# Every fifth weight operand of the first half in ScalarE's two copy tiles, and one accumulation there on VectorE

## The chip, the core and the metric

The kernel runs on one core of a Trainium2 chip. The core has a matrix engine (PE, with its weight loads shown apart as PEld), a vector engine (DVE), a scalar engine (ACT), GpSimd (POOL), and SyncE (SP), on whose queue all of this kernel's transfers are issued. The engines run side by side, each in its own fixed order of instructions, and wait for one another through semaphores. The metric is the time of one execution on the device, in microseconds (us).

## What is computed

A residual trunk of one layer over 2048 tokens of width 1024, in float32. Two mixers run on the normalised input and are projected back; that takes the first 540 us or so and the change leaves it alone. Then comes the SwiGLU block, 2816 wide, and a final norm:

```
h = rmsnorm(h_res, norm_ffn_g[l])
ff = jax.nn.silu(h @ ffn_w1[l]) * (h @ ffn_w3[l])
h_res = h_res + ff @ ffn_w2[l]
return rmsnorm(h_res, final_norm_g)
```

## The kernel before, in words

**Two halves.** The 2048 tokens are four chunks of 512. The SwiGLU block runs twice, over two chunks each: the first half (`hf == 0`) and the second (`hf == 1`). All that follows is about the first half.

**Seven products instead of eight.** Each 2x2 block product is formed by Strassen-Winograd's scheme: seven products per 2x2 block, with sums and differences of the weight quarters (`t1` to `t4`, made on POOL by `comb`, lines 605 and 703) and of the activations. There are eleven blocks of the inner width (`NP`, index `j`). For a block, `ffn1` runs twice (gate and up, tiles `ps`, operands `h_hi`, `h_lo`) and `ffn2` once (tiles `pY`, `pX`, `pZ`, `pV`, operands `f_hi`, `f_lo`). In the loop, `ffn_up(j)` comes first, and then `ffn2(j)` and `ffn_gate(j + 1)` step in turn, so one pass of the loop, here called a cycle, is 21 products of 12 matmuls each. Ten such cycles follow each other.

**Two float32 parts.** Each operand is split into a rounded part and a rest: `split` copies on ACT (line 226) and subtracts on DVE (line 236). A product uses three matmuls per tile (`mm3`, lines 239 to 241): high by high, high by low, low by high. The third needs the weight's low part, so it waits for DVE.

**Where split weights live.** In the first half a weight operand is loaded raw (`load_raw`, line 210, six buffers) or combined on POOL, then split by `split_kept` into a tile `w_hl` that holds both parts. This ring (`wsp`) has four buffers: a fifth split can start only when PE has finished the product four operands back. The split is also stored to DRAM (line 205, 512 KB) for the second half, which reads it back. `t3` and `t4` go through a tag with one buffer (`r1`): the next of them can be formed only when DVE has split the one before.

**The two tiles of ACT's copies.** The tag `e` has two buffers of 512 columns. In `add` (line 712 on), a product's bank is added to its accumulator either by DVE straight from the bank (line 715, `by == "V"`), or by an ACT copy into a tile `e` and a POOL addition (line 719, `by == "P"`). In the first half of the kernel before, only the fifth product of `ffn2` (tiles `pZ`, accumulator `G`) goes by ACT and POOL.

**What sets the order.** A scheduler puts the instructions of each engine in order ahead of the run, from priorities, dependences and its own costs. Weight splits are given priority (`AHEAD`), so they stand as early as a buffer is free. The order of a queue is then fixed; an instruction that waits holds up all behind it on its engine.

Of the kernel before, what the change touches and what calls it, by code (L numbers as in the profile page):

```python
# [9 lines left out]
F32 = mybir.dt.float32  # L10
F32R = mybir.dt.float32r
# [6 lines left out]
P = 128  # L18
# [17 lines left out]
AHEAD = 400  # L36
# [36 lines left out]
def trunk(ctx: ExitStack, tc: tile.TileContext, xT, w_io, w13, w2, gates, pool_w, w_inT, vecs,  # L73
          consts, outT):
    nc = tc.nc
# [90 lines left out]
    c13_d = dram.tile([NP, 2, 7, P, 2, W], F32, name="c13_d")  # L166
    c2_d = dram.tile([NP, 7, P, 2, W], F32, name="c2_d")
# [8 lines left out]
    def t2(name, tag, shape=(P, T), dt=F32):  # L176
        return pool.tile(list(shape), dt, name=name, tag="t2_" + tag, bufs=N_T2[tag])

    def wsp(name, shape):
        return pool.tile(list(shape), F32R, name=name, tag="wsp", bufs=N_WSP)  # L180
# [3 lines left out]
    def kept(cache):  # L184


        n_kept[0] += 1
        if n_kept[0] % 7 in (1, 3, 5):
            parts = []
            for i in range(2):  # L190
                t = pool.tile([P, W], F32, name="w_kept", tag="raw", bufs=N_RAW)
                nc.sync.dma_start(t, cache[:, i])
                parts.append(t.bitcast(F32R))
            return parts
        t = pool.tile([P, 2, W], F32, name="w_kept2", tag="wsp", bufs=N_WSP)
        nc.sync.dma_start(t, cache)
        t = t.bitcast(F32R)
        return t[:, 0], t[:, 1]

    def split_kept(src, cache, prepare=AHEAD, eng=None):  # L200

        w_ = wsp("w_hl", (P, 2, W))
        with tc.high_priority(prepare):
            split(w_[:, 0], w_[:, 1], src, eng)
        nc.sync.dma_start(cache, w_.bitcast(F32))
        return w_[:, 0], w_[:, 1]
# [6 lines left out]
    def bank(name):  # L213
        return psum.tile([P, T], F32, name=name, tag="mm", bufs=4)
# [10 lines left out]
    def copy_a(out, in_):  # L225
        return nc.scalar.activation(out, in_, AF.Copy)  # L226
# [6 lines left out]
    def split(hi, lo, src, eng=None):  # L233

        copy_a(hi, src)
        (eng or nc.vector).tensor_tensor(lo, src, hi.bitcast(F32), ALU.subtract)  # L236
# [356 lines left out]
    def ffn1(hf, j, w, ops, s, after):  # L593
# [12 lines left out]
            return t  # L606

        def product(n, ps, a, b, fresh):
            wh, wl = split_kept(b, c13_d[j, w, n]) if hf == 0 else kept(c13_d[j, w, n])
            for kk in range(NB):  # L610
                col = slice(kk * P, kk * P + P)
                mm3(ps, wh[:, col], wl[:, col], a[0][:, kk], a[1][:, kk],
                    fresh and kk == 0, kk == NB - 1, skip_group_check=True)
# [23 lines left out]
        Z, V = bank("ps"), bank("ps")  # L637
# [52 lines left out]
    def ffn2(hf, j, s, acc, G):  # L690
# [13 lines left out]
            return t  # L704

        def product(n, banks, a, b, fresh):
            wh, wl = split_kept(b, c2_d[j, n]) if hf == 0 else kept(c2_d[j, n])
            for dp, ps in enumerate(banks):
                col = slice(P * dp, P * (dp + 1))
                mm3(ps, wh[:, col], wl[:, col], a[0], a[1], fresh, True, skip_group_check=True)  # L710

        def add(banks, dst, by):
            for dp, ps in enumerate(banks):
                if by == "V":
                    nc.vector.tensor_tensor(dst[dp], ps, dst[dp], ALU.add)  # L715
                else:
                    e = t2("e", "e")
                    copy_a(e, ps)
                    nc.gpsimd.tensor_tensor(dst[dp], dst[dp], e, ALU.add)  # L719
# [11 lines left out]
        g = [G[:, dp] for dp in range(NB)]  # L731
# [26 lines left out]
        s2 = half(ALU.subtract, s1, a11)  # L758
        Z = banks("pZ")
        product(4, Z, operand(s2), tt2, True)  # L760
        add(Z, g, "P")
        yield
        V = banks("pV")
        product(5, V, operand(s1), t1, True)
# [207 lines left out]
```

## Time and profile before

| what | value |
|---|---|
| median of 3 runs | 1911.29 us (1910.66 to 1914.16) |
| profiled execution, its own time | 1915.5 us |
| its span, first to last instruction | 1913.7 us |
| PE busy | 1826.2 us, 95% |
| DVE busy | 1350.9 us, 71% |
| ACT busy | 728.8 us, 38% |
| POOL busy | 803.6 us, 42% |

The busy shares are means over stages that differ: the first half of the SwiGLU block lies between about 549 and 1240 us, the second between about 1240 and 1862 us. PE's busy time counts an instruction from start to end, and matmuls overlap, so the number of matmuls in a stretch tells more of its speed than the busy share. Times in the rows are microseconds from the span's start; a row's bracket is the idle time of its engine just before and what ended it.

### The profile page before, as it was taken

Reading aid. Unit: us, or ns where it says so; the run is one execution under the profiler, and the core shown is the slowest. Engines: PE = TensorE matmul, PEld = TensorE weight load, DVE = VectorE, ACT = ScalarE, POOL = GpSimd, SP = SyncE. Lnnn points to the kernel's source line nnn. Section 1 sums busy time; section 2 is a strip of 40 time slices with the busy share of each in tenths; the row PEclk is TensorE's granted clock in tenths of the full one; section 3 lists DMA queues with packets and bytes.
Section 4 is the critical chain, followed back from the end, with each engine's and each line's share of the span. In section 5 each row is a group of like instructions: output and inputs, shape, how many; then the busy total and the mean of one; then the engine's idle time right before and its main releaser. Section 6 shows DMA issues by size and latency. Waiting matters only on the chain.

```text
span 1913.7 us, 23347 instructions
## 1 busy us (share of the span) xinstructions
PE 1826.2 (95%) x8016; PEld 1479.8 (77%) x8016; DVE 1350.9 (71%) x2080; ACT 728.8 (38%) x1216; POOL 803.6 (42%) x557
## 2 busy tenths in 40 slices
PE   7998999999988999999999999799999999999996
PEld 5787887787767777778777787678888888888885
DVE  7588599895768779878898778984544554544558
ACT  5554546352334434333343334532322223322223
POOL 3361623342234545345453556352433333433373
PEclk9999999999989999999999999899999999999998
DMA  9874954576987676666766667777555555555542
GB/s 322 316 254 171 345 207 168 176 269 238 362 330 288 218 257 226 235 228 239 257 228 227 229 240 274 294 226 280 194 192 198 192 193 183 194 197 190 198 172 88
DMA packets 160837, 444.68 MB, mean 232 GB/s; under 512 B 17872, under 2 KB 20048, under 8 KB 155728
## 3 DMA queue, kind: packets, MB, share of 16 engines
q1 hardware_dynamic: 160720, 443.20, 65.2%
q8 instruction: 63, 1.03, 0.2%
q14 instruction: 54, 0.44, 0.1%
HBM read 275.36 MB, written 167.77 MB: 232 GB/s over the span
## 4 chain that ended last, share of the span: by engine, by line
PE 66%; DVE 21%; DMA 5%; issue 4%; POOL 2%; ACT 1%; SPq 0%; DVEq 0%; ACTq 0%; POOLq 0%
PE ps L241 15%; PE ps L239 15%; PE ps L240 15%; DVE w_hl L236 2%; PE pV L239 2%; PE pV L240 2%; PE pX L240 2%; PE pX L239 2%; PE pX L241 2%; PE pV L241 2%; DMA w_kept<-cio_d 1%; DVE sf L728 1%; DVE h_lo L236 1%; DVE xc L424 1%; DVE acc L715 1%
## 5 line engine op out<-in xcount | busy, mean ns | idle before, releaser
L241 PE MATMUL ps<-h_hi,w_hl 128*128 128x512 f32 x616 | 246.5, 401 | 15.8 <-DVE w_hl L236 15.4
L239 PE MATMUL ps<-h_hi,w_hl 128*128 128x512 f32 x616 | 244.5, 399 | 13.9 <-DVE u L645 9.4
L239 PE MATMUL ps<-h_hi,w_kept 128*128 128x512 f32 x616 | 241.8, 393 | 4.4 <-DVE sf L728 1.9
L240 PE MATMUL ps<-h_lo,w_hl 128*128 128x512 f32 x616 | 244.1, 396 | 0.0
L240 PE MATMUL ps<-h_lo,w_kept 128*128 128x512 f32 x616 | 241.4, 392 | 2.1 <-DVE h_lo L236 2.1
L241 PE MATMUL ps<-h_hi,w_kept 128*128 128x512 f32 x616 | 239.3, 392 | 0.0
L719 POOL TENSOR_TENSOR G<-G,e 128x512 f32<-128x512 f32 x116 | 168.5, 1476 | 107.0 <-ACT e L226 107.0
L295 POOL TENSOR_TENSOR sq<-sq 128x512 f32<-128x512 f32 (+1 forms) x71 | 103.7, 1465 | 158.1 <-ACT sq L292 156.4
L641 POOL TENSOR_TENSOR u<-u,u 128x512 f32<-128x512 f32 x44 | 66.8, 1517 | 227.7 <-DVE u L639 227.6
L241 PEld LDWEIGHTS ps<-h_hi,w_hl 128*128 128x128 f32 x616 | 117.6, 191 | 51.0 <-DVE w_hl L236 25.6
L239 PEld LDWEIGHTS ps<-h_hi,w_hl 128*128 128x128 f32 x616 | 117.7, 191 | 44.9 <-ACT w_hl L226 9.4
L236 DVE TENSOR_TENSOR f_lo<-sf,f_hi 128x512 fp32r<-128x512 f32 x80 | 75.3, 942 | 105.6 <-PE pZ L240 41.5
L605 POOL TENSOR_TENSOR t<-raw 128x512 f32<-128x512 f32 x44 | 65.7, 1497 | 186.0 <-DVE w_hl L236 92.3
L239 PEld LDWEIGHTS ps<-h_hi,w_kept 128*128 128x128 f32 x616 | 116.1, 188 | 31.2 <-DVE sf L728 2.3
L715 DVE TENSOR_TENSOR acc<-pV,acc 128x512 f32<-128x512 f32 x160 | 106.5, 687 | 46.7 <-PE pV L241 46.2
L240 PEld LDWEIGHTS ps<-h_lo,w_hl 128*128 128x128 f32 x616 | 117.7, 191 | 25.3 <-DVE h_lo L236 0.2
L240 PEld LDWEIGHTS ps<-h_lo,w_kept 128*128 128x128 f32 x616 | 116.0, 188 | 27.5 <-DVE h_lo L236 2.5
L241 PEld LDWEIGHTS ps<-h_hi,w_kept 128*128 128x128 f32 x616 | 116.1, 188 | 25.5 <-DMA w_kept<-c_d 0.3
L236 DVE TENSOR_TENSOR w_hl<-raw,w_hl 128x512 fp32r<-128x512 f32 x120 | 120.4, 1005 | 19.1 <-ACT w_hl L226 17.6
L226 ACT ACTIVATE f_hi<-sf 128x512 fp32r<-128x512 f32 x80 | 50.1, 627 | 188.2 <-DVE sf L728 150.6
L226 ACT ACTIVATE w_hl<-t 128x512 fp32r<-128x512 f32 x96 | 60.5, 630 | 145.8 <-PE ps L241 55.4
L226 ACT ACTIVATE w_hl<-raw 128x512 fp32r<-128x512 f32 x140 | 85.7, 623 | 77.4 <-PE ps L241 59.4
(359 smaller groups left out, 4499.3 us busy)
## 6 DMA issues: line engine op xcount, KB each, us to landing
c_d<-w_hl SPq DMA_DIRECT2D x228, 512.0 KB, 2.9
w_kept<-c_d SPq DMA_DIRECT2D x130, 512.0 KB, 3.6
w_kept<-c_d SPq DMA_DIRECT2D x196, 256.0 KB, 3.4
w_kept<-cio_d SPq DMA_DIRECT2D x68, 512.0 KB, 3.7
raw<-w SPq DMA_DIRECT2D x132, 256.0 KB, 3.3
w_kept<-cio_d SPq DMA_DIRECT2D x104, 256.0 KB, 3.2
cio_d<-w_hl SPq DMA_DIRECT2D x40, 512.0 KB, 4.9
h_lo<-h_d SPq DMA_DIRECT2D x14, 1024.0 KB, 9.8
```

Source lines behind the costliest of these rows:

```text
L226: return nc.scalar.activation(out, in_, AF.Copy)
L236: (eng or nc.vector).tensor_tensor(lo, src, hi.bitcast(F32), ALU.subtract)
L239: i = nc.tensor.matmul(ps, wh, xh, start=first, stop=False, **kw)
L240: nc.tensor.matmul(ps, wh, xl, start=False, stop=False, **kw)
L241: nc.tensor.matmul(ps, wl, xh, start=False, stop=last, **kw)
L295: eng.tensor_tensor(total, total, sq, ALU.add)
L424: nc.vector.scalar_tensor_tensor(x[:, d:], u[:, 0:T - d], tap(3 - d), x[:, d:], ALU.mult, ALU.add)
L605: nc.gpsimd.tensor_tensor(t, a, b, ALU.subtract)
L641: nc.gpsimd.tensor_tensor(u3, u3, u2, ALU.add)
L715: nc.vector.tensor_tensor(dst[dp], ps, dst[dp], ALU.add)
L719: nc.gpsimd.tensor_tensor(dst[dp], dst[dp], e, ALU.add)
L728: nc.vector.tensor_tensor(out, a, b, op)
```

## The change

Of the operands that `ffn1` and `ffn2` split in the first half, every fifth now goes into two tiles of the tag `e`, one for each part, and is stored by two transfers of 256 KB. The accumulation of `pZ` into `G`, which used those tiles, is done there by DVE from the bank.

```diff
-    def split_kept(src, cache, prepare=AHEAD, eng=None):
+    n_split = [0]
+
+    def split_kept(src, cache, prepare=AHEAD, eng=None, five=False):
+        n_split[0] += five
+        if five and n_split[0] % 5 == 0:
+            parts = t2("w_e", "e", dt=F32R), t2("w_e", "e", dt=F32R)
+            with tc.high_priority(prepare):
+                split(*parts, src, eng)
+            for i, part in enumerate(parts):
+                nc.sync.dma_start(cache[:, i], part.bitcast(F32))
+            return parts
...
-            wh, wl = split_kept(b, c13_d[j, w, n]) if hf == 0 else kept(c13_d[j, w, n])
+            wh, wl = split_kept(b, c13_d[j, w, n], five=True) if hf == 0 else kept(c13_d[j, w, n])
...
-            wh, wl = split_kept(b, c2_d[j, n]) if hf == 0 else kept(c2_d[j, n])
+            wh, wl = split_kept(b, c2_d[j, n], five=True) if hf == 0 else kept(c2_d[j, n])
...
-        add(Z, g, "P")
+        add(Z, g, "P" if hf else "V")
```

The scheduler orders the first half anew; up to it every engine's order is the same. In the changed kernel the lines behind `split_kept` have numbers higher by 11, so line 236 is 247 there. Three places follow.

DVE in the cycle whose `ffn_up` ends near 778 us. Before, the last two rows ahead of these are `u_6714<-ps` (the addition at line 639) and the split of the first combined weight of `ffn2`, `t_6854`. `t_6910` is the second one's, `t_6936` that of the gate product that runs beside them:

```order
L679 TENSOR_TENSOR c<-ps,u_6714 128x512
L236 TENSOR_TENSOR w_hl<-raw,w_hl 128x512
L680 TENSOR_TENSOR s<-s,c 128x512
L645 TENSOR_TENSOR u_6738<-ps,u_6738 128x512
L728 TENSOR_TENSOR sf<-s 128x512
L236 TENSOR_TENSOR f_lo<-sf,f_hi 128x512
L236 TENSOR_TENSOR w_hl<-t_6910,w_hl 128x512
L728 TENSOR_TENSOR sf<-s 128x512
L236 TENSOR_TENSOR f_lo<-s,f_hi 128x512
L728 TENSOR_TENSOR sf<-sf,s 128x512
L679 TENSOR_TENSOR u_6714<-ps,u_6714 128x512
L236 TENSOR_TENSOR w_hl<-t_6936,w_hl 128x512
```

The same place now, where the three combined weights are `t_6860`, `t_6916` and `t_6944`, and the addition is `u_6718<-ps`:

```order
L247 TENSOR_TENSOR w_hl<-t_6860,w_hl 128x512
L650 TENSOR_TENSOR u_6718<-ps,u_6718 128x512
L247 TENSOR_TENSOR w_e<-t_6916,w_e 128x512
L690 TENSOR_TENSOR c<-ps,u_6718 128x512
L247 TENSOR_TENSOR w_hl<-raw,w_hl 128x512
L691 TENSOR_TENSOR s<-s,c 128x512
L739 TENSOR_TENSOR sf<-s 128x512
L656 TENSOR_TENSOR u_6742<-ps,u_6742 128x512
L247 TENSOR_TENSOR w_hl<-t_6944,w_hl 128x512
```

The first combined weight has moved ahead of the addition, and the gate product's weight stands seven rows behind the addition, where it stood thirteen behind. The first row of `acc<-pY` stands sixteen rows behind the addition in both.

DVE where `pZ` and `pV` are accumulated, one cycle later. Before:

```order
L639 TENSOR_TENSOR u_6896<-ps,u_6896 128x512
L236 TENSOR_TENSOR w_hl<-raw,w_hl 128x512
L666 TENSOR_TENSOR s<-ps,u_6896 128x512
L236 TENSOR_TENSOR f_lo<-sf,f_hi 128x512
L236 TENSOR_TENSOR w_hl<-raw,w_hl 128x512
L645 TENSOR_TENSOR u_6954<-ps,u_6954 128x512
L715 TENSOR_TENSOR acc<-pV,acc 128x512
L236 TENSOR_TENSOR w_hl<-raw,w_hl 128x512
```

And now:

```order
L247 TENSOR_TENSOR w_e<-raw,w_e 128x512
L677 TENSOR_TENSOR s<-ps,u_6902 128x512
L247 TENSOR_TENSOR w_hl<-raw,w_hl 128x512
L726 TENSOR_TENSOR G<-pZ,G 128x512 x3
L656 TENSOR_TENSOR u_6962<-ps,u_6962 128x512
L247 TENSOR_TENSOR f_lo<-sf,f_hi 128x512
L726 TENSOR_TENSOR G<-pZ,G 128x512
L247 TENSOR_TENSOR w_hl<-raw,w_hl 128x512
L726 TENSOR_TENSOR acc<-pV,acc 128x512
```

Four additions have come in ahead of the first `acc<-pV`.

POOL at the end of the loop, where `fold` (line 774) adds `G` to twelve accumulator tiles and the last block's combined weights (`t_10302`, `t_10341`, `t__10343`, `t_10345`) are formed. Before:

```order
L641 TENSOR_TENSOR u_10014<-u_10014,u_9956 128x512
L719 TENSOR_TENSOR G<-G,e 128x512 x2
L774 TENSOR_TENSOR acc<-acc,G 128x512
L719 TENSOR_TENSOR G<-G,e 128x512
L774 TENSOR_TENSOR acc<-acc,G 128x512
L719 TENSOR_TENSOR G<-G,e 128x512
L774 TENSOR_TENSOR acc<-acc,G 128x512 x6
L605 TENSOR_TENSOR t_10345<-raw,t__10343 128x512
```

And now:

```order
L616 TENSOR_TENSOR t__10351<-raw,t_10349 128x512
L652 TENSOR_TENSOR u_10024<-u_10024,u_9966 128x512
L785 TENSOR_TENSOR acc<-acc,G 128x512 x8
L616 TENSOR_TENSOR t_10353<-raw,t__10351 128x512
L785 TENSOR_TENSOR acc<-acc,G 128x512 x4
```

The four additions of `G` are gone from between the line before and the last combined weight; the eight of `fold` still stand ahead of it.

## Rows read from the trace of the kernel before

**Rows 1.** Page, part 1: busy time, share and instructions of each engine.

```profile
PE 1826.2 (95%) x8016; PEld 1479.8 (77%) x8016; DVE 1350.9 (71%) x2080; ACT 728.8 (38%) x1216; POOL 803.6 (42%) x557
```

**Rows 2.** Stretches: width; busy PE, PEld, DVE, ACT, POOL; clock; DMA share; GB/s.

```profile
549.00:629.00 80.00, 69.34 (x268) 53.93 (x269) 68.64 (x97) 32.92 (x57) 35.04 (x21) 0.89 0.75 273
...
689.00:749.00 60.00, 58.89 (x253) 46.72 (x252) 49.18 (x68) 23.15 (x41) 29.31 (x19) 1.00 0.65 237
...
1169.00:1240.00 71.00, 59.91 (x248) 47.15 (x246) 61.95 (x83) 35.34 (x63) 39.60 (x27) 0.93 0.79 293
...
1302.00:1862.00 560.00, 560.00 (x2455) 460.66 (x2454) 270.52 (x368) 154.06 (x261) 209.86 (x153) 1.00 0.57 195
```

**Rows 3.** Waits of PE's weight loads, 629 to 1169 us: total, times, longest.

```profile
PEld ps L241 <- DVE w_hl L236: 17.1, 18, 1.4
PEld pY L239 <- DVE acc L715: 7.1, 18, 0.5
PEld ps L239 <- ACT w_hl L226: 3.8, 9, 0.5
PEld pV L239 <- ACT e L226: 1.8, 7, 0.3
```

**Rows 4.** Timeline of one cycle's busiest stretch, 777 to 794 us.

```profile
777.49 1.31 POOL L605 TENSOR_TENSOR t<-raw 128x512 f32<-128x512 f32 x1 [9.16 <-DMA raw<-w]
777.51 0.63 ACT L226 ACTIVATE w_hl<-t 128x512 fp32r<-128x512 f32 x1 [4.47 <-PE ps L241]
777.92 0.69 DVE L639 TENSOR_TENSOR u<-ps,u 128x512 f32<-128x512 f32 x1 [4.16 <-PE ps L241]
...
780.46 1.74 POOL L605 TENSOR_TENSOR t__7030<-raw,t 128x512 f32<-128x512 f32 x1
780.98 1.77 DVE L680 TENSOR_TENSOR s<-s,c 128x512 f32<-128x512 f32 x1
...
785.15 1.00 DVE L236 TENSOR_TENSOR f_lo<-sf,f_hi 128x512 fp32r<-128x512 f32 x1 [0.70 <-ACT f_hi L226]
...
790.90 0.19 PEld L241 LDWEIGHTS ps<-h_hi,w_hl 128*128 128x128 f32 x1 [1.39 <-DVE w_hl L236]
...
793.80 0.19 PEld L239 LDWEIGHTS pY<-f_hi,w_hl 128*128 128x128 f32 x1 [0.31 <-DVE acc L715]
```

**Rows 5.** Timeline around the accumulation of pZ, 753 to 759 us.

```profile
753.59 6.48 POOL L719 TENSOR_TENSOR G<-G,e 128x512 f32<-128x512 f32 x4
...
754.30 1.57 DVE L236 TENSOR_TENSOR w_hl<-raw,w_hl 128x512 fp32r<-128x512 f32 x1
...
756.52 0.69 DVE L715 TENSOR_TENSOR acc<-pV,acc 128x512 f32<-128x512 f32 x1
...
758.21 0.69 DVE L236 TENSOR_TENSOR w_hl<-raw,w_hl 128x512 fp32r<-128x512 f32 x1 [1.00 <-ACT w_hl L226]
```

**Rows 6.** Instructions of tiles e and G, 629 to 1169 us: ns minimum/median/maximum.

```profile
L226 ACT ACTIVATE e<-pZ x36: 597/600/602, 630.9 to 1116.6; 128x512 f32<-128x512 f32 x36
...
L719 POOL TENSOR_TENSOR G<-G,e x36: 1278/1741/1839, 632.7 to 1118.2; 128x512 f32<-128x512 f32 x36
L715 DVE TENSOR_TENSOR G<-pX,G x36: 673/677/689, 680.7 to 1165.1; 128x512 f32<-128x512 f32 x36
```

**Rows 7.** Timeline of the first half's beginning, 566 to 572 us.

```profile
566.48 0.28 PEld L241 LDWEIGHTS ps<-h_hi,w_hl 128*128 128x128 f32 x1 [2.86 <-DVE w_hl L236]
...
571.84 0.19 PEld L239 LDWEIGHTS ps<-h_hi,w_hl 128*128 128x128 f32 x1 [1.39 <-ACT w_hl L226]
```

**Rows 8.** Timeline of the first half's end, 1183 to 1211 us.

```profile
1183.36 7.97 POOL L774 TENSOR_TENSOR acc<-acc,G 128x512 f32<-128x512 f32 x6
...
1193.28 1.08 DVE L236 TENSOR_TENSOR w_hl<-t,w_hl 128x512 fp32r<-128x512 f32 x1 [6.28 <-ACT w_hl L226]
...
1210.29 0.29 PEld L239 LDWEIGHTS ps<-h_hi,w_hl 128*128 128x128 f32 x1 [8.31 <-ACT h_hi L226]
```

**Rows 9.** Page, part 6: transfers, KB each, median us to landing.

```profile
c_d<-w_hl SPq DMA_DIRECT2D x228, 512.0 KB, 2.9
```

## The prediction

> **What bounds the kernel now.** I first read the busy time of each engine [rows 1]: PE is busy for 95% of the span, which seems to leave nothing. But matmuls overlap and a busy PE need not be at its peak, so I turned to the table by stretches and counted matmuls [rows 2]. In the second half, from 1302 to 1862 us, PE starts 2455 matmuls in 560 us: 4.38 per us, with DVE busy for less than half of the time. That is my measure of full speed. One cycle of the first half (689 to 749 us) holds 253 matmuls; at full speed they take 57.7 us, and they take 60, so **a cycle loses 2.3 us**. The nine cycles from 629 to 1169 us lose 20.6 us. The beginning (549 to 629 us) has 268 matmuls, worth 61.1 us, in 80: 18.9 us lost. The end (1169 to 1240 us) has 248, worth 56.6 us, in 71: 14.4 us lost. The change can win from these 54 us and from nothing else, since the second half keeps its code.
>
> What the losses are, the waits of the weight loads tell [rows 3]. Over the nine cycles they wait 17.1 us for a weight's low part from DVE (`w_hl`, line 236), 7.1 us for DVE's additions of `pY`, 3.8 us for ACT's copies of weights and 1.8 us for ACT's copies of `pZ`: 29.8 us, or 3.31 a cycle. PE loses only 2.29, because loads run ahead of matmuls; so a wait of 1 us costs PE 0.69. DVE's split is 57% of the sum.
>
> Why the split is late, the timeline of one cycle's busiest stretch shows [rows 4]. At 777.51 us ACT begins the copy of a combined weight, after 4.47 us of waiting for PE: the ring of four is full, and only the product four operands back gives a buffer free. From then on DVE has a queue: `u<-ps,u` (line 639) at 777.92, then twelve instructions, then the gate product's weight as the thirteenth. PE gets to its low part at 790.90 after a wait of 1.39 us, 12.3 us after `u` has ended. Thirteen rows in 12.3 us are 0.95 each, not 0.69: `s<-s,c` takes 1.77 at 780.98 beside POOL's 1.74 at 780.46, and DVE stands still for 0.70 at 785.15. A little later PE waits 0.31 for the addition of `pY`. So what binds is DVE's backlog, and the full ring lets it form.
>
> **The extra weights in the cycle.** Of the 21 operands of a cycle four or five now go into the `e` tiles, so while one is there, a split starts a product earlier. The order on DVE shows what follows at this place: the first combined weight is split ahead of `u` instead of behind it, and the gate product's weight stands seven rows behind `u` instead of thirteen. At 0.95 a row it ends 5.7 us sooner; the wait it causes is 1.39. So the split's waits should go: 57% of 2.29 is **1.3 us a cycle**, my value. The upper end: DVE's additions and the `pZ` copies stop being late too, 26.0 of 29.8, or 2.0 us. The lower end: the first addition of `pY` stands sixteen rows behind `u` in both orders. If these rows take as long as before but for the wait of 0.70, PE stops there instead, and the gain is 0.69 of 0.70, or 0.5 us. I take 1.3 since the long rows should shrink: fewer additions of POOL stand beside them. Nine cycles give **11.8 us** (4.5 to 18).
>
> **The accumulation of `pZ`.** Gone per cycle are four copies on ACT of 0.60 us, on an engine that is idle for most of the cycle [rows 2], and four additions on POOL of 1.74 [rows 6]. New are four on DVE; the same form for `pX` takes 0.677 us, so 2.7 us per cycle. Against it stands what DVE does beside POOL's run of these additions [rows 5]: a split that begins at 754.30 takes 1.57 us, the one at 758.21, of the same form, 0.69: 0.88 saved. Before the second one DVE is idle for 1.00 us. That leaves 0.8 us, ahead of `acc<-pV`, whose lateness PE hardly feels: waits at `pV` are 1.8 us in all nine cycles [rows 3], and they were for ACT's copies, which go. I take **nothing** for it; uncovered it would cost 0.69 of 0.8, 0.6 us a cycle, or 5 us.
>
> Only one of the two splits lies deep in the POOL run, while an addition from a bank at 756.52 takes 0.69 beside it [rows 5]. The Trainium skill ("SBUF — State Buffer", section "Who interferes with whom") gives a rule for that: a DVE instruction with two SBUF inputs contends with a GpSimd instruction that reads SBUF, and one of them blocks fully, while one with at most one SBUF input does not contend. By the rule a two-input row could lose up to a whole POOL instruction, and without the four additions DVE would gain 0.9 for each of them, 3.5 us against the 2.7 added, so moving them would be a small gain of DVE and not the cost it looks. The rows agree on 1.57 and on 0.69 from a bank, and disagree on the split at 758.21, which stays at 0.69 with POOL still in its run; so my sum takes the 0.88 once.
>
> **Stores.** The fifth operands are stored by two transfers of 256 KB instead of one of 512. The issues go to SP, which has no other work; a store of 512 KB lands 2.9 us (median) after its issue [rows 9], and the transfers' share of the cycle is 0.65 [rows 2]. The bytes are the same. I take nothing; what it would cost if that is wrong is the slower rival below.
>
> **The beginning.** There the weight loads wait 2.86 us at 566.48 for a split and 1.39 at 571.84 for a copy [rows 7], and the granted clock over the stretch is 0.89, against 1.00 in the cycles [rows 2], that is, part of it was at the lower level. These are the first weights of the first block, when the ring has just filled; in the new order one of the two splits stands thirteen rows and the other five rows earlier on DVE. Both waits gone are **4.3 us**. From below: nothing, if PE then waits for the next raw load. From above: 0.11 of 80 us at the lower clock is 8.8 us; if half of that stood behind these two waits, 8.7 in all.
>
> **The end.** `fold` keeps POOL busy, six additions in 7.97 us from 1183.36; behind them comes the last combined weight, whose split on DVE starts at 1193.28 after 6.28 us of idling, and at 1210.29 PE stands 8.31 us for the next operand [rows 8]. The order on POOL has lost the four additions of `G`; two of them stood among those of `fold`, at 1.74 each [rows 6]: 3.5 us sooner. At most DVE's whole idle time goes, 6.28. I take the middle, **4.9 us**. Bounds: 8.3, if the wait vanishes, and 1.0 lost, if DVE's four additions there come ahead of something late.
>
> **The sum**: 11.8 + 0 + 0 + 4.3 + 4.9 = 21.0 us. The profiled execution took 1915.5 us (span 1913.7), 4.2 above the median of 1911.3; the stretches belong to it, and I take their difference over unchanged. 1915.5 - 21.0 = 1894.5, and for the median **1890.3 us**.
>
> **Rivals.**
>
> A, the forecast: the split's waits go, 1890.3.
>
> B, **the wait only changes its owner**: PE stops at the additions of `pY`, since DVE has all the rows it had and four more. For it: sixteen rows on both sides, and a wait of 0.31 that is already there [rows 4]. Against it: POOL's run, which stretched DVE's rows, is shorter by 7 us a cycle. It gives 0.5 in nine cycles, 4.5 us, half of the beginning, 2.1, and 3.5 at the end: 10.1 us, or 1901. With `pZ` uncovered besides, 5 us less: 1906.
>
> C, **the raw loads come later**: slower. All transfers share SP's queue, in order. A store waits there until its low part is written, and the raw loads behind it wait along; splits that DVE now makes sooner or later shift them. POOL had waited 9.16 us for a raw tile until 777.49, and formed the weight only 0.43 us before `u` began [rows 4]: there is no slack. If in each cycle the loads slip by one long DVE row (1.77), less the 0.43, then 1.34 x 9 = 12.1 us are lost; with the beginning's 4.3 won and the end lost to the same queue, 1919. It decides from a slip of 0.43 us on, if the split's waits don't shrink. Against it: SP is idle most of the time and 0.35 of the transfer time is free.
>
> D, **it does not act**: the slot that the `e` tiles add is taken back by what is formed just in time (`t3`, `t4` through their single buffer, raw tiles), splits wait for these, and DVE's added rows eat the rest. 1911. Against it: the waits of ACT for PE (4.47 us) show that operands were there and buffers weren't.
>
> **How the numbers follow.** A 0.60, B 0.22, C 0.09, D 0.09. The prediction is A's 1890.3. A's far bounds are 18 + 8.7 + 8.3 = 35 us, 1876. A and B hold 0.82, so the range ends with B and the uncovered `pZ`: 1876 to 1907. A measurement of this kernel tells about 0.2%, 3.8 us, from no change. Faster by more: A and B, 0.82; within: D, 0.09; slower: C, 0.09.
>
> **What would show it.** In the new profile 253 matmuls of a cycle should take 58.7 us rather than 60, and the waits of weight loads for `w_hl` should fall from 17.1 to under 5 us. If those for `acc` at `pY` rise above 12 us in their place, B is right. The split beside `pZ` should take about 0.7 us; if the waits at `pV` rise, `pZ` was not covered. At the beginning the waits of 2.86 and 1.39 should be gone and the clock above 0.89; at the end DVE's idle time before the last combined weight should be under 3 us and the wait of 8.31 under 5. POOL's waits for raw tiles growing beyond 9.16 us at that place would show C. If the cycles are still 60 us long, the reading that the ring lets DVE's backlog form is wrong.

## The result and the profile after

The changed kernel takes 1901.99 us (median of 6 runs, 1899.06 to 1904.43), the kernel before, beside it, 1913.64 (1910.66 to 1914.7): a ratio of 0.9941, interval 0.9930 to 0.9952, or 11.6 us less. Forecast were 21.0 less, 1890.3. A second set of runs, after_again below, gave 0.9936 (0.9922 to 0.9951).

The time is split best by work done, not by the clock on the wall, since the changed kernel reaches each stage earlier. Both programs start the same number of matmuls in each stage, so I cut both traces at the same matmuls: the 2350th (the SwiGLU block begins), the 2602nd, the 4870th (nine cycles of 252 later) and the 5374th (what follows takes equally long in both). The part from the 4870th to the 5374th, 504 matmuls, is called the passage below: the end of the first half and the beginning of the second.

Busy time by these stretches, columns as in [rows 2]; first the kernel before:

```profile
555.95:627.69 71.74, 63.23 (x253) 49.54 (x252) 60.38 (x85) 30.70 (x53) 30.57 (x18) 0.93 0.72 263
627.69:1168.27 540.58, 530.55 (x2270) 421.24 (x2269) 444.56 (x602) 209.46 (x360) 264.19 (x171) 1.00 0.66 236
1168.27:1302.61 134.34, 117.96 (x505) 93.92 (x504) 110.30 (x151) 59.36 (x104) 76.71 (x51) 0.95 0.78 276
```

And the changed kernel:

```profile
553.19:621.66 68.47, 61.83 (x253) 47.03 (x252) 60.83 (x84) 30.51 (x53) 31.37 (x18) 0.97 0.77 276
621.66:1150.09 528.43, 523.45 (x2269) 425.00 (x2268) 455.25 (x640) 187.73 (x324) 195.39 (x135) 1.00 0.67 242
1150.09:1288.48 138.39, 120.65 (x506) 95.65 (x504) 113.68 (x156) 57.40 (x99) 70.55 (x47) 0.94 0.79 278
```

The first number behind the two times is the length. The beginning is 3.3 us shorter, the nine cycles 12.2, and the passage is 4.0 **longer**. What follows (602.4 us in both, to the last matmul) is equal. The sum is -11.4, which is what the medians show.

The passage holds two stretches that went opposite ways. They meet where PE first uses a weight of the second half (`w_kept`), at the same matmul of the products in both kernels: at 1240.34 us before, which is where the forecast's end stops [rows 2], and at 1216.07 now. Before, then changed:

```profile
1168.27:1240.34 72.07, 60.65 (x252) 47.75 (x250) 63.02 (x85) 36.22 (x64) 39.94 (x27) 0.93 0.79 290
1240.34:1302.61 62.27, 57.31 (x254) 46.16 (x255) 47.27 (x67) 23.15 (x41) 36.77 (x25) 0.97 0.78 260
...
1150.09:1216.07 65.98, 61.38 (x260) 48.41 (x258) 60.63 (x82) 31.65 (x54) 34.62 (x23) 0.97 0.89 318
1216.07:1288.48 72.41, 59.27 (x249) 47.23 (x248) 53.05 (x75) 25.75 (x46) 35.92 (x24) 0.91 0.70 242
```

The end of the first half is 6.1 us shorter and the start of the second half 10.1 us longer. A second profile of the same program (after_again) has 64.50 and 71.95 us, and two more kernels whose engines have the same order up to that point have 65.90 and 67.81 for the end. So the end is known to 2 or 3 us from single profiles, and the loss behind it is clear of that. In the start of the second half the granted clock is 0.91 instead of 0.97, so more of it ran at the lower of the clock's two levels: 0.09 of 72.41 us against 0.03 of 62.27, which makes at most 4.6 of the 10.1 us (an estimate from these rows, since part of it passes while PE stands). The stops of PE make the rest.

In the nine cycles the waits of the weight loads, 29.8 us before [rows 3], are these now (total, times, longest):

```profile
PEld ps L250 <- DVE u L656: 3.4, 6, 1.3
PEld pY L250 <- ACT f_hi L237: 2.6, 2, 1.3
PEld pX L250 <- DVE G L726: 1.7, 2, 0.8
```

The wait of 17.1 us for DVE's split is gone, and so is that of 7.1 for the additions of `pY`. In the passage PE itself waits like this:

```profile
PE ps L251 <- DVE h_lo L247: 4.3, 1, 4.3
PE ps L250 <- ACT h_hi L237: 3.6, 1, 3.6
PE p L250 <- ACT f_hi L237: 2.6, 1, 2.6
PE ps L250 <- DMA w_kept<-c_d: 2.6, 1, 2.6
```

The stop of 8.31 us at the end of the first half [rows 8] has shrunk: at the same place in the count of matmuls PE now waits 2.6 us for `f_hi`. The three other waits lie in the start of the second half, for its operands `h_hi` and `h_lo` and for one of its weights. These operands are sums of activation quarters: `h_s124` forms them on DVE (lines 596 to 600, `a`), ACT copies them, DVE subtracts (`h_lo`). DVE is where they are late. Three more things fall into the passage: the first half's final norm, whose squares are summed (`add_sq`, line 306, on POOL), whose root is taken in small steps on 128x4 elements (`nr_`, on DVE), and which then scales the output (line 857 on DVE, 855 on POOL).

The stores in two pieces (page, part 6: KB each, median us to landing) land as soon after their issue as those of 512 KB did [rows 9]:

```profile
c_d<-w_e SPq DMA_DIRECT2D x88, 256.0 KB, 2.9
```

### The profile page after: what moved, and what is told of

Its sections match the earlier page's. It is cut to its first block, busy times and chain, and to the rows that moved or that the text cites. A ratio compares the mean times of both kernels' runs of the same rounds, so it can differ in the third digit from the quotient of the medians.

```text
span 1899.4 us, 23387 instructions
## 1 busy us (share of the span) xinstructions
PE 1817.1 (96%) x8016; PEld 1480.4 (78%) x8016; DVE 1364.0 (72%) x2120; ACT 705.6 (37%) x1176; POOL 727.8 (38%) x517
## 4 chain that ended last, share of the span: by engine, by line
PE 70%; DVE 19%; DMA 5%; issue 3%; POOL 2%; ACT 1%; SPq 0%; DVEq 0%; POOLq 0%; ACTq 0%
PE ps L250 16%; PE ps L251 16%; PE ps L252 16%; PE pX L250 2%; PE pX L251 2%; PE pX L252 2%; PE pV L250 2%; PE pV L251 2%; PE pV L252 2%; PE pY L250 2%; PE pY L252 2%; PE pY L251 2%; DVE w_hl L247 1%; DVE xc L435 1%; DVE h_lo L247 1%
## 5 line engine op out<-in xcount | busy, mean ns | idle before, releaser
L250 PE MATMUL ps<-h_hi,w_hl 128*128 128x512 f32 x496 | 196.8, 398 | 3.9 <-ACT w_hl L237 2.4
L252 PE MATMUL ps<-h_hi,w_hl 128*128 128x512 f32 x496 | 194.8, 396 | 3.8 <-DVE w_hl L247 3.8
L251 PE MATMUL ps<-h_lo,w_hl 128*128 128x512 f32 x496 | 196.2, 396 | 0.5 <-DVE h_lo L247 0.5
L652 POOL TENSOR_TENSOR u<-u,u 128x512 f32<-128x512 f32 x44 | 63.0, 1433 | 237.7 <-DVE u L650 231.9
L730 POOL TENSOR_TENSOR G<-G,e 128x512 f32<-128x512 f32 x76 | 103.7, 1386 | 110.6 <-ACT e L237 110.6
L250 PEld LDWEIGHTS ps<-h_hi,w_hl 128*128 128x128 f32 x496 | 94.5, 191 | 26.6 <-ACT w_hl L237 2.4
L252 PEld LDWEIGHTS ps<-h_hi,w_hl 128*128 128x128 f32 x496 | 94.2, 190 | 26.9 <-DVE w_hl L247 6.1
L251 PE MATMUL ps<-x_lo,w_kept 128*128 128x512 f32 x288 | 112.8, 394 | 1.5 <-DVE x_lo L354 1.5
L237 ACT ACTIVATE w_hl<-raw 128x512 fp32r<-128x512 f32 x121 | 74.9, 624 | 105.0 <-PE ps L252 70.0
L250 PE MATMUL ps<-x_hi,w_kept 128*128 128x512 f32 x288 | 112.5, 393 | 1.1 <-DVE u_g L406 1.1
L252 PE MATMUL ps<-x_hi,w_kept 128*128 128x512 f32 x288 | 112.9, 393 | 0.0
L251 PEld LDWEIGHTS ps<-h_lo,w_hl 128*128 128x128 f32 x496 | 94.6, 191 | 21.4 <-DVE h_lo L247 0.8
```

Of the source, the lines that this page charges most:

```text
L250: i = nc.tensor.matmul(ps, wh, xh, start=first, stop=False, **kw)
L251: nc.tensor.matmul(ps, wh, xl, start=False, stop=False, **kw)
L252: nc.tensor.matmul(ps, wl, xh, start=False, stop=last, **kw)
L652: nc.gpsimd.tensor_tensor(u3, u3, u2, ALU.add)
```

## Experiments

Two questions: is it the operands in the `e` tiles that shorten the cycles, or the additions taken off POOL? And why did the passage get longer? All times are medians with the kernel before run beside them; where one profile is compared with another, I take stretches cut at the same matmuls. Differences of a microsecond or two between medians of different sets of runs say nothing.

### Which part shortens the cycles

**v_only**: the accumulation alone.

```diff
-        add(Z, g, "P")
+        add(Z, g, "P" if hf else "V")
```

> The kernel before with one part of the change: in the first half pZ is added to G by VectorE from the bank; no weight operand goes into the e tiles, the ring keeps its four buffers. Theory 1 (the extra buffer is what speeds the cycles): the cycles stay near 60.1 us per 252 matmuls, 59.6 to 60.5, and the whole time is within 5 us of the kernel before. Theory 2 (fewer POOL additions beside VectorE, and no gain from buffers): a cycle takes about 58.8 us, as in the changed kernel, and the time is about 11 us below the kernel before.

1908.45 us against 1914.52, ratio 0.9973 (0.9962 to 0.9984). The nine cycles take as long as before, 540.15 against 540.58 us, and the old wait is all there; stretches first, then waits:

```profile
627.13:1167.28 540.15, 529.86 (x2270) 421.62 (x2269) 459.59 (x638) 189.23 (x324) 200.55 (x135) 1.00 0.65 236
1167.28:1298.33 131.05, 116.08 (x506) 92.74 (x504) 116.34 (x155) 56.90 (x100) 71.56 (x47) 0.97 0.79 279
```

```profile
PEld ps L241 <- DVE w_hl L236: 17.4, 18, 1.4
PEld pY L239 <- DVE acc L715: 7.1, 18, 0.5
```

Relieving POOL gives the cycles nothing; theory 2 falls. The time is 6.1 us lower, a little more than the 5 that theory 1 allowed. Of that the profile shows 3.3 us in the passage: 1.3 in the end (70.81 us) and 2.0 in the start of the second half (60.24).

**pool_back**: the changed kernel with 36 POOL instructions put back into the cycles.

```diff
         add(Z, g, "P" if hf else "V")
+        if hf == 0:
+            for dp in range(NB):
+                nc.gpsimd.tensor_tensor(g[dp], g[dp], ones.to_broadcast((P, T)), ALU.mult)
```

> The changed kernel, and per block four multiplications of G by one on GpSimd, of 128x512 elements, that stand in for the four additions of G it has lost. Theory 1 (buffers): the cycles keep most of their gain, 58.8 to 59.3 us on the mean, and the time is at most 4 us above the changed kernel's. Theory 2 (relief of GpSimd): the cycles go back towards 60.1 us and the time rises by 9 us or more.

1908.21 against 1914.52, ratio 0.9974 (0.9963 to 0.9984). The cycles keep the whole gain though POOL has its 36 instructions back (240.6 us busy, against 264.2 in the kernel before):

```profile
626.12:1154.63 528.51, 523.22 (x2270) 424.95 (x2269) 461.33 (x640) 187.96 (x324) 240.64 (x171) 1.00 0.68 242
```

The time is 5 us worse than the changed kernel's difference to its own kernel before, more than the 4 expected, but the trace puts that outside the cycles: the passage takes 141.6 us, its end as much as in the kernel before (71.97), and the beginning 69.8. So the operands in the `e` tiles are what shortens the cycles: theory 1, from both sides. They bring a further buffer and, with it, a new order of the engines; no run has the buffer in the old order.

**phase0, phase2, phase4**: where in the cycle. In the changed kernel the cycles are not equal: cut every 252 matmuls, they take 59.9, 58.0, 57.9, 59.1, 59.4, 59.3, 58.0, 57.9 and 59.1 us. Since 21 leaves 1 on division by 5, the place of the `e` operands walks through the cycle and returns after five. Three kernels hold the place fixed (and leave the last block's operands in the ring: `use` is false there). The line of phase2:

```diff
-        if five and n_split[0] % 5 == 0:
+        if five and use and (n_split[0] - 8) % 21 in (2, 7, 12, 17):
```

> Four operands of each cycle go into the e tiles, always the same: with the 21 operands of a cycle numbered from 0 in the order of the program, 0, 5, 10 and 15; none in the last block. In the changed kernel the place walks through the cycle with a period of five cycles, and the cycles in which it began at 0 took 57.9 to 58.0 us. Theory 1 (the place in the cycle decides whether a cycle loses): all nine cycles take 57.9, 521 us together, against 525.9 in old_end, and the time is 4 to 6 us below old_end's. Theory 2 (the unequal cycles have another cause, such as arrivals of transfers): about 526 us again and within 2 us of old_end.

> As phase0, with operands 4, 9, 14 and 19 of each cycle. In the changed kernel cycles that began at 4 took 57.9 us. Theory 1 (the place decides): 521 us for nine cycles, 4 to 6 us below old_end. Theory 2: 526 us, within 2 us of old_end.

> As phase0, with operands 2, 7, 12 and 17 of each cycle. In the changed kernel the cycle that began at 2 took 59.4 us. Theory 1 (the place decides): nine cycles at 59.4, 535 us, and 7 to 10 us above old_end. Theory 2 (another cause): 526 us, within 2 us of old_end.

Busy time of the nine cycles in phase0, phase4 and phase2:

```profile
625.68:1158.46 532.78, 526.21 (x2270) 426.13 (x2268) 455.17 (x640) 189.40 (x324) 194.25 (x135) 1.00 0.68 241
...
623.24:1145.62 522.38, 521.87 (x2269) 425.55 (x2268) 441.34 (x638) 189.09 (x324) 191.62 (x135) 1.00 0.69 246
...
619.21:1140.56 521.35, 521.35 (x2270) 425.90 (x2269) 442.85 (x640) 191.98 (x324) 194.80 (x135) 1.00 0.69 246
```

The place decides: in phase2 all nine cycles take 57.95 us (the last 57.8) and no weight load waits at all, in phase4 they take 58.0 on the mean, in phase0 58.2 to 61.9. But my reading of which place is good was wrong: phase2 was to be the slow one and phase0 fast. I had given a cycle's time to the place in that cycle. Perhaps the orders of the neighbouring cycles have a part in it; why the one place is better is not shown here. Times: phase0 1902.73 (ratio 0.9946, 0.9933 to 0.9960), phase4 1901.10 (0.9934, 0.9920 to 0.9947), phase2 1894.39 (0.9900, 0.9887 to 0.9914). Phase4 has short cycles and no better a time: its passage takes 141.6 us.

### What lengthens the passage

**old_end**: the last block's operands stay in the ring.

```diff
-            wh, wl = split_kept(b, c13_d[j, w, n], five=True) if hf == 0 else kept(c13_d[j, w, n])
+            wh, wl = split_kept(b, c13_d[j, w, n], five=j < NP - 1) if hf == 0 else kept(c13_d[j, w, n])
```

> The changed kernel, but the last block of the first half is as in the kernel before: its operands all go through the ring of four, and its pZ by ScalarE and GpSimd. Theory 1 (the passage between the halves lost 4 us by the order that the change gave it): the 504 matmuls of the passage take about 134 us again rather than 138.4, and the time is 3 to 6 us below the changed kernel's. Theory 2 (whoever arrives early at the passage waits there for the second half's operands, whatever the order): they take 137 us or more, and the time is within 2 us of the changed kernel's.

One part of that edit has no effect: the last block has no `pZ` (its `ffn2` is another function), so its accumulations are DVE's everywhere. 1896.04 against 1914.52, ratio 0.9913 (0.9898 to 0.9929); the passage takes 135.2 us and the cycles 525.9. That fits theory 1, but phase2 and phase4 leave the last block's operands in the ring too, and their passages take 140.8 and 141.6. So it is not the operands as such. What old_end shares with the kernel before, and not with these, is the order on DVE at the beginning of the second half.

**store_behind**: SyncE's queue. In the changed kernel SP waits 19.8 us with the first store of the finished chunk (`outT<-acc`) for DVE's scaling, from the end of this row to the start of the next:

```profile
1221.60 0.80 SPq L192 DMA_DIRECT2D w_kept<-c_d  x2
1242.27 4.21 SPq L864 DMA_DIRECT2D outT<-acc  x5
```

Five weight loads of the second half that the kernel before issued ahead of that store now stand behind it. The edit puts them ahead again:

```diff
+            if hf and (j, w, n) == (0, 1, 5):
+                for i in stores:
+                    issue_after(i, last["load"])
...
-                    nc.sync.dma_start(outT[2 * hf + t, h, :, k], y)
+                    i = nc.sync.dma_start(outT[2 * hf + t, h, :, k], y)
+                    if not hf:
+                        stores.append(i)
```

> The changed kernel, but on SyncE's queue the eight stores of the first half's first normalised chunk stand behind the second half's first weight loads (as they do in the kernel before) instead of ahead of five of them. Theory 1 (the queue held these loads back by some 20 us, and PE waited for them): no wait of PE for w_kept near the passage, its 504 matmuls in about 133.5 us rather than 138.4, and the time 4 to 6 us below the changed kernel's. Theory 2 (VectorE's chain for the second half's operands sets the passage, and the loads were late beside it): at most 2 us.

1899.50 against 1914.52, ratio 0.9926 (0.9909 to 0.9944), which overlaps the changed kernel's interval. The passage takes 137.55 us instead of 138.39: theory 2. PE's wait for a weight fell from 2.6 to 1.0 us, but 0.8 us of passage is less than two profiles of one program differ by, so a price of the late loads is not shown.

**norm_ahead and norm_behind**: DVE's order. Here is DVE in the changed kernel where the second half's operands are done (each row: start, length, engine, line):

```profile
1238.53 0.69 DVE L247 TENSOR_TENSOR h_lo<-a,h_hi 128x512 fp32r<-128x512 f32 x1 [0.70 <-ACT h_hi L237]
1240.36 5.29 DVE L857 SCALAR_TENSOR_TENSOR acc<-acc,vec,r 128x512 f32<-128x512 f32 x3 [1.13 <-ACT r L237]
1245.57 0.15 DVE L274 TENSOR_SCALAR nr_m<-cols 128x4 f32<-128x4 f32 x1
1245.75 1.07 DVE L276 TENSOR_SCALAR nr_i<-nr_m 128x4 int32<-128x4 int32 x1
1246.86 1.21 DVE L280 SCALAR_TENSOR_TENSOR nr_a<-nr_i 128x4 f32<-128x4 f32 x1
...
1249.55 0.68 DVE L650 TENSOR_TENSOR u<-ps,u 128x512 f32<-128x512 f32 x1
```

Three scalings of the first half's output (`acc`) and eleven small steps of its second norm (`nr_`) stand between the last `h_lo` and the addition `u<-ps,u` of the second half's first gate product: 10.3 us. In the kernel before the addition came at once:

```profile
1260.14 0.69 DVE L236 TENSOR_TENSOR h_lo<-a,h_hi 128x512 fp32r<-128x512 f32 x1
1260.74 0.69 DVE L639 TENSOR_TENSOR u<-ps,u 128x512 f32<-128x512 f32 x1
1261.46 0.69 DVE L666 TENSOR_TENSOR s<-ps,u 128x512 f32<-128x512 f32 x1
1262.63 4.16 DVE L846 SCALAR_TENSOR_TENSOR acc<-acc,vec,r 128x512 f32<-128x512 f32 x3 [0.48 <-ACT r L226]
```

The same split runs through all kernels up to here: in before, v_only and old_end this addition stands one to four rows behind the last `h_lo`, and the passage takes 131 to 135 us; in the changed kernel, store_behind, pool_back and the three phases eight to fifteen rows, and it takes 137.5 to 141.6 (136.5 in the second profile of the changed kernel). To see whether the one causes the other, the order is turned round in both: in norm_ahead on the kernel before, in norm_behind on store_behind.

```diff
-        nc.vector.tensor_tensor(u2, Z, u2, ALU.add)
+        add = nc.vector.tensor_tensor(u2, Z, u2, ALU.add)
+        if hf and not j and not w:
+            issue_after(add, last_nr["root"])
```

> The mirror image, on the kernel before: u2 of the second half's first gate product is put behind the root of the first half's second chunk, fourteen rows behind the last h_lo, where it had stood one behind. No weight operand goes into the e tiles. Theory 1: the passage takes 138 to 142 us rather than 134.3, and the time is 4 to 8 us above the kernel before. Theory 2: within 2 us of it.

1919.55 against 1913.75, ratio 1.0032 (1.0019 to 1.0044); its passage:

```profile
1168.91:1308.31 139.40, 118.91 (x505) 94.53 (x504) 112.62 (x153) 59.30 (x104) 76.45 (x51) 0.94 0.79 282
```

That is 5.1 us longer, and the time 5.8: as theory 1 has it. Of the 5.1 us, 4.9 lie in the start of the second half (67.17 against 62.27). But PE does not stop at the addition there. Its one long stop is at `bc`, the matmuls that spread the root of the first half's second chunk. Here it is, first in norm_ahead, then in the changed kernel:

```profile
1272.77 0.55 PE L282 MATMUL bc<-cst,nr_y 128*128 128x128 f32 x1 [6.11 <-DVE nr_y L273]
...
1249.78 0.35 PE L293 MATMUL bc<-cst,nr_y 128*128 128x128 f32 x1 [1.17 <-DVE nr_y L284]
```

With the rows on DVE the scheduler has moved `bc` too: in norm_ahead it stands 28 matmuls earlier on PE than in the kernel before, at the place that it has in the changed kernel. So the run prices the norm's place on both engines together, and its 6.11 us are not the changed kernel's 1.17. In pool_back and the three phases, whose `bc` stands later, PE does stop for the addition itself, 1.7 to 2.6 us. In norm_behind the loop over the held rows is `issue_after(i, add)`:

> store_behind, and on VectorE the first half's final norm (its first chunk's three scalings and its second chunk's root) stands behind the first addition of the second half's first gate product (u2<-ps) instead of ahead of it. In the changed kernel fourteen such rows stand between the last operand of the second half and that addition; in the kernel before, in v_only and in old_end it stands one to four rows behind the last operand. Theory 1 (these rows ahead of u2 hold PE's second half back): the 504 matmuls of the passage take 130 to 134 us rather than the 137.5 of store_behind, u2 within 3 us of the last h_lo rather than 11, and the time 4 to 7 us below store_behind's. Theory 2 (u2 is late for another reason and the rows only fill its wait): 136.5 or more, within 1.5 us.

1897.73 against 1913.75, ratio 0.9917 (0.9903 to 0.9930). The passage takes 134.3 us, 3.2 less than store_behind's and 4.1 less than the changed kernel's. Up to the second half's first weight PE, DVE, ACT and POOL have the same order in norm_behind as in store_behind; there its profile is 1.9 us longer, and behind it 5.1 us shorter (66.51 against 71.65). `bc` stands 35 matmuls later on PE, and PE no longer waits for it. The medians do not show the 5 us: they are 1.0 us apart in their distance to before, where 4 to 7 were expected. Waits for `h_hi` and `h_lo` of 1.3 and 4.3 us are still there.

**no_sq and before_no_sq**: why these operands are late at all. In the changed kernel DVE's rows of that chain are long, and POOL is adding up the squares for the first half's final norm at the time (DVE, then POOL):

```profile
1222.11 1.78 DVE L247 TENSOR_TENSOR h_lo<-a,h_hi 128x512 fp32r<-128x512 f32 x1
1223.81 1.77 DVE L600 TENSOR_TENSOR a<-h_lo,a 128x512 f32<-128x512 f32 x1
```

```profile
1216.91 9.79 POOL L306 TENSOR_TENSOR sq<-sq 128x512 f32<-128x512 f32 x6 [1.81 <-ACT sq L303]
```

```diff
-                total = add_sq(total, y, "s" if end else "f", nc.vector if sq_on[k] == "V" else nc.gpsimd)
+                sq = add_sq(total if end else None, y, "s" if end else "f", ...)
+                total = sq if end or k == 0 else total
```

> The changed kernel without the fourteen additions of squares that GpSimd makes for the final norm of the first half (left out; the norm there uses the first square alone). Theory 1 (VectorE's chain for the second half's operands sets the passage, and GpSimd stretches its instructions there from 0.68 to 1.2 to 1.78 us): the 504 matmuls of the passage take 130 to 133 us rather than 138.4, and the time is 5 to 8 us below the changed kernel's. Theory 2 (the arrival of transfers or PE's order sets it): 137 us or more, within 2 us.

> The kernel before without the fourteen additions of squares on GpSimd for the first half's final norm (left out, as in no_sq). no_sq on the changed kernel brought the passage from 138.4 to 124.4 us. Theory 1 (both kernels' passages are held by VectorE's chain for the second half's operands, stretched by these additions; the changed kernel's 4 us on top come from its order): 122 to 128 us here rather than 134.3, so nearly the same for both. Theory 2 (the changed kernel alone suffers, since it comes to the passage earlier and so meets these additions): 131 or more.

no_sq: 1889.96 against 1914.65 (0.9876, 0.9863 to 0.9890). before_no_sq: 1907.40 against 1912.97 (0.9971, 0.9960 to 0.9983). Their passages:

```profile
1150.96:1275.33 124.37, 115.60 (x506) 92.66 (x505) 99.85 (x156) 55.85 (x99) 49.86 (x33) 0.99 0.88 313
...
1168.68:1296.66 127.98, 115.29 (x506) 92.69 (x505) 100.00 (x153) 59.02 (x104) 55.65 (x37) 0.97 0.83 292
```

14.0 us less in the changed kernel, twice what theory 1 expected, and 6.4 less before. So the additions hold both, and the changed kernel more; without them its passage is the shorter one, and the start of the second half takes 60.2 us in it and 58.6 in the kernel before. before_no_sq ended at the rim of what theory 1 allowed, and its DVE order changed as well (three scalings ahead of `u`), so the 6.4 is not the additions' price alone. The same holds for the 14.0: without the additions the norm's rows come earlier.

**after_v and phase2_nb_v**: the additions on DVE, nothing left out. **phase2_nb** and **phase2_nb_pe**: phase2 in norm_behind's order, and then with the squares summed by PE.

```diff
-NOT_LAST = tuple((t, 0, T, "PPPPPPPP", (0, 2, 3, 5, 6)) for t in (1, 0))
+NOT_LAST = tuple((t, 0, T, "VVVVVVVV", (0, 2, 3, 5, 6)) for t in (1, 0))
```

> The changed kernel once more, unchanged, beside the others of this call, so that they are compared on one chip. All theories: 10 to 13 us below the kernel before, a passage of 137 to 140 us, and cycles of 527 to 529 us.

> The changed kernel with the fourteen additions of squares of the first half's final norm on VectorE instead of GpSimd; nothing is left out. They cost VectorE 14 x 0.68 = 9.5 us and should spare it about 9 us of stretched rows. Theory 1 (the stretch is what costs): the passage takes 130 to 136 us rather than 138.4, the time 3 to 8 us below the changed kernel's. Theory 2 (the work itself counts, on whichever engine): 138 or more.

> phase2 (operands 2, 7, 12 and 17 of each cycle in the e tiles, none in the last block) with the order of norm_behind. phase2 had its nine cycles at 57.95 us and a passage of 140.8. Theory 1: passage 132 to 135, the time 5 to 8 us below phase2's, about 1888. Theory 2: 139 or more, within 2 us of phase2.

> phase2_nb with these additions on VectorE. Theory 1: passage 128 to 134 us rather than 136.6, time 3 to 8 us below phase2_nb's, about 1889. Theory 2: no gain.

> phase2_nb, and the squares of the first half's final norm are summed by PE (32 small matmuls per chunk into one bank) instead of by seven additions per chunk on GpSimd; nothing is left out. If GpSimd's additions stretch VectorE in the passage (no_sq without them took 124.4 instead of 138.4), the passage takes 124 to 129 us and the time is 5 to 9 us below phase2_nb's. If PE's 64 small matmuls wait for ScalarE's squares and hold up PE's queue, the time is equal or higher.

| kernel | us | kernel before | ratio, interval | passage, us |
|---|---|---|---|---|
| after_again | 1900.68 | 1912.97 | 0.9936 (0.9922 to 0.9951) | 136.5 |
| after_v | 1891.01 | 1912.97 | 0.9880 (0.9864 to 0.9896) | 128.6 |
| phase2_nb | 1895.95 | 1913.75 | 0.9903 (0.9890 to 0.9917) | 136.6 |
| phase2_nb_v | 1882.41 | 1912.97 | 0.9839 (0.9824 to 0.9854) | 125.0 |
| phase2_nb_pe | 1897.31 | 1913.75 | 0.9908 (0.9893 to 0.9924) | 147.4 |

after_again's passage is a little below the 137 to 140 expected. after_v, on the same chip, is 9.7 us faster, more than the 3 to 8 expected. The passage, after_v's first, then that of phase2_nb_v:

```profile
1152.18:1280.75 128.57, 118.19 (x505) 94.87 (x505) 111.73 (x169) 56.45 (x99) 48.80 (x33) 0.96 0.83 283
...
1145.15:1270.18 125.03, 116.59 (x505) 93.90 (x504) 108.52 (x167) 56.69 (x99) 50.02 (x33) 0.97 0.81 289
```

DVE does 13 instructions more than in the changed kernel's passage (169 against 156) in 2 us less. So it is the collision that costs, not the work: theory 1. The order has moved as well: in after_v the addition stands seven rows behind the last `h_lo`, not fifteen, and `bc` 39 matmuls later on PE. phase2_nb and phase2_nb_v keep the two apart, since the addition stands three rows behind in both: there the start of the second half falls from 69.79 to 61.20 us, and the ratio from 0.9903 to 0.9839.

phase2_nb did not do what theory 1 expected of it (a passage of 132 to 135 us, 5 to 8 us of time). Its addition stands three rows behind the last `h_lo`, its passage is 136.6 us, 4.2 below phase2's, and its ratio is the same (0.9903 and 0.9900). Of the 4.2, 2.2 lie in the end, where the two programs have the same order; 2.0 are left for the norm's place. phase2_nb_pe brought nothing: the time is that of phase2_nb. Cut at the same matmuls of the products its passage is 10.8 us longer, in a profiled execution that was the slowest of five. PE has 112 small matmuls more there and waits nowhere for the squares, but the granted clock over the passage is 0.88, in phase2_nb 0.93. **phase2_nb_v beats both kernels**: 30.6 us, 1.6%, below the kernel before.

The two stretches of the passage, in us, of the kernels that the account rests on:

| kernel | end of the first half | start of the second half |
|---|---|---|
| before | 72.07 | 62.27 |
| v_only | 70.81 | 60.24 |
| pool_back | 71.97 | 69.60 |
| changed, and its second profile | 65.98, 64.50 | 72.41, 71.95 |
| norm_ahead (before, norm first) | 72.23 | 67.17 |
| store_behind, then norm_behind | 65.90, 67.81 | 71.65, 66.51 |
| phase2, then phase2_nb | 69.01, 66.80 | 71.81, 69.79 |
| after_v | 65.72 | 62.85 |
| before_no_sq, no_sq | 69.39, 64.20 | 58.59, 60.17 |

## Why the prediction was right and wrong

| term | forecast | measured |
|---|---|---|
| nine cycles | -11.8 (-4.5 to -18) | -12.15 |
| accumulation of `pZ` in them | 0 | -0.4 (v_only), within the line above |
| stores in two pieces | 0 | 2.9 us to landing, as before |
| beginning | -4.3 (0 to -8.7) | -3.27 |
| end, to the second half's first weight | -4.9 (+1.0 to -8.3) | -6.09 |
| start of the second half | 0, "keeps its code" | +10.14 |
| sum | -21.0 | -11.37 |

**What bound the cycles** was read rightly as far as the runs go: with every fifth operand out of the ring the waits for DVE's split are gone, and v_only and pool_back show from both sides that the operands did it and not POOL. That it was the fuller ring, and not the new order alone, is not shown; the phases, with the same two tiles at other places, take 521 to 533 us. The mean cycle was forecast at 58.7 us and is 58.7; that it is a mean of 57.9 and 59.4 was not seen, nor that the place could be chosen, which is worth another 7 us (528.4 to 521.35).

**The accumulation** cost nothing, as taken. DVE has 36 additions more in v_only's cycles than before, 24.4 us at 0.677, and 15.0 us more busy time (459.59 against 444.56): 9.3 us came back from shorter rows, 1.0 a cycle where I took 0.88 once. The rule of the Trainium skill ("SBUF — State Buffer", section "Who interferes with whom") as I had worked it out, 3.5 a cycle, was too much there. In the passage the trace agrees with the rule: the long rows of 512 columns have two SBUF inputs and take up to 1.77 beside a POOL instruction that reads SBUF, instead of 0.69.

**The beginning**: right in direction, and due to the operands in the `e` tiles (v_only's beginning takes 71.9 us, as before). The waits of 2.86 and 1.39 are gone, but others took their place: the weight loads wait 11.7 us there in all, before 11.8. The clock is 0.97 against 0.93 over the same matmuls. In norm_behind and after_v, the same program up to there, it was 0.93 too, and they took 69.5 and 69.7 us; so some 2 us are the change's, and the rest of the 3.3 fits the clock of that execution.

**The end** came inside its bounds, 6.1 us shorter against 4.9 forecast. The reading of it was right in part. PE's own row for the stop names what it waited for, and it is no operand but DVE's addition `u` (line 645), which stood in DVE's backlog:

```profile
1210.32 0.77 PE L239 MATMUL ps<-h_hi,w_hl 128*128 128x512 f32 x1 [7.92 <-DVE u L645]
```

The additions of `G` off POOL bring 1.3 us of it alone (v_only), the operands with POOL's instructions put back 0.1 (pool_back), both together 6.1, each in a single profile. That v_only's whole passage is 3.3 us shorter, near the 3.5 that I had from the two additions among `fold`'s, is luck.

**The step that failed** is the sentence that the change can win from these 54 us "and from nothing else, since the second half keeps its code". It put the start of the second half at nothing. The code stayed, but not the order nor the time at which PE comes there: this stretch took 72.41 us instead of 62.27. Those 10.1 us are the whole miss: without them the sum would have been -21.5, against -21.0 forecast. I had stopped reading at the wait of 8.31 and had not asked what PE would meet next.

What it met were the operands of the second half, which DVE forms in rows that POOL stretches. PE stops there for 13.2 us in all, 5.7 before: 3.6 and 4.3 for `h_hi` and `h_lo`, 2.6 for a weight, 1.5 for an addition and 1.2 for the root. POOL's additions of squares are the larger cause: with them on DVE the stretch is 8.6 us shorter at the same place of the norm (phase2_nb to phase2_nb_v), and in after_v it takes 62.85 us, as in the kernel before. The other is the order, which was there to be read: fourteen rows of the final norm stood ahead of the second half's first addition, and `bc` 28 matmuls earlier on PE. Turning this round costs 4.9 us of this stretch in norm_ahead and brings 5.1 in norm_behind, 2.0 in phase2_nb; only norm_ahead's median shows it clear of noise. The two causes overlap, and how the 10.1 us divide between them is not settled. The place of the stores cost little, if anything.

Of the **rivals**, B gave 1901, close to what was measured, but not by its mechanism, so that is luck: the waits for additions at `pY` fell from 7.1 to nearly nothing instead of rising above 12. C (raw loads slipping behind stores) did not show in the cycles. The nearest thing to the truth, a wait that changes its owner, I had placed in the cycle; it took place behind the first half.

## What to carry to other kernels

When a change makes a stage faster, price also the stage behind it: follow the engine that gained to the next thing it waits for, and read there, too, what the new order puts ahead of what. In a hand-over between two stages, look whether work that finishes the old one (a norm, its stores) stands ahead of the first operation that the new one needs, on every engine that both use. Where rows of an engine take twice their usual time, look at the rows of the other engines at the same moment; here, taking that other work onto the slowed engine was a gain for it.

## What was not expected of the hardware

- Fourteen additions moved from GpSimd to VectorE made VectorE's busy time shorter: 113.7 us with 156 instructions in the changed kernel's passage, 111.7 with 169 in after_v's. Even steps on 128x4 elements were stretched: `nr_i` took 1.07 us and `nr_a` 1.21 beside GpSimd's scalings, where the rows of the same kind behind them take 0.16.
- The same program up to the 2350th matmul, whichever kernel followed, took between 551.5 and 557.7 us in the profiled executions of these kernels. Two single profiles are therefore compared from a common matmul on, not from the start.
